# A fixed order on PE for output projection and routing, and the first context pair's product on POOL

## The chip, the cores and the metric

One core of a Trainium2 chip. The engines are PE (matrix products and transposes, into PSUM), DVE and ACT (element by element, both reach PSUM), POOL (element by element in SBUF, and indirect transfers) and SP (issues most transfers). Each engine runs its own list of instructions in order and waits at semaphores for the others. The metric is the device time of one execution in microseconds; lower is better.

## What is computed

One step of a two-layer backbone for two sets of tokens, 512 latent tokens and 128 context tokens, of width 1024. A layer is

```
x <- LN(ALPHA * x + gate1 * (mixers(modulate(x)) @ w_out))
x <- LN(ALPHA * x + gate2 * experts(modulate(x)))
```

The mixers are latent attention, a pooling mixer and a short convolution; their concatenated output (1024 wide) goes through one output projection `w_out`. The experts are 16 SwiGLU units of inner width 512: `(silu(u @ w_gate) * (u @ w_up)) @ w_down`. Routing is by choice of the experts: the router gives each token softmax weights over 16 experts, and each expert takes the tokens with the largest weights, 64 of the latent set and 16 of the context set, each set routed alone. What an expert gives for a token is scaled with that weight and added to the token's row.

## The kernel before

All numbers of lines are those of the kernel before. The 640 tokens are five tiles of 128: the context tile (CTX) and latent tiles 0 to 3. Everything below happens in each of the two layers; the places named are layer 0's.

**Output projection** (`out_proj`, from L776). `project(t, half)` (L844) makes 512 of the 1024 output columns of a tile: eight steps k, each of three products 128x512 (`mm3`, L229: inputs and weights are split in a high and a low part, `mh`/`ml` and `wo..h`/`wo..l`). The weights come as four quarters, `wo00`, `wo01` (for half 0), `wo10`, `wo11` (half 1); each is split on the way (L226 on ACT makes the high part, L227 the low part, on DVE or POOL). The sum stands in a PSUM tile `ps_o` (three buffers). DVE multiplies it with the gate (L859), adds it to the row tile `xa` (L861, in layer 1 L864) and takes statistics (L867); after half 1 it makes the mean and variance, POOL the power -0.5 (`bsd`, L285), DVE the product of mean and `bsd` (`bnb`, L322).

**Routing of a tile.** `turn(t, g)` transposes half g of `xa` on PE (L881), ACT copies it to `u2` (L883), PE multiplies it with the router's weights (L887, bank `ps_rt`). `route(t)`: ACT copies the partial sums (L896), PE folds them (L898), DVE and ACT make the softmax `rex` (L900 to L906), PE transposes it (L907), DVE copies it to `affl` (L909). ACT then normalises `xa` (L323) and stores it in DRAM as `zrow` (L911). `residual(t)` multiplies and adds on POOL (L337, L338) in place and starts the accumulator's row (L842); it has to wait for the store of `zrow`.

**Context tokens.** After the context tile's routing, `route_ctx` picks each expert's 16 tokens, two gathers (`xsc`) bring their rows, eight transposes each (`transpose8`) and a modulation on ACT (L261) give `xc`.

**End of the stage.** `route_late` (L946 on) does the last half of tile 3 with `fill(n)` between: n steps of the first pair of experts' product for context tokens (`context`, four products a step into `ps_gc`, eight steps in all). Then the top-k of the latent set on DVE (`topk`, L976 to L980, eight rounds), `route_lat` (DVE, then PE transposes the list `ldup` at L989, DVE writes the indices `lgi`, L1041) and the gather of the first pair's rows `xsl` on POOL's queue (L961).

**First pair of experts** (`experts`, j = 0): `ctx_hidden` (ACT makes `sc`, the SiLU of the gate half of `ps_gc`, L1164, for which it loads a table; DVE multiplies it with the up half, `hc`, L1166, held behind `lgi`), `ctx_turn` (PE `ps_hcT`, ACT `hcT`, L1175), `ctx_rows` (16 products into `ps_dc`, and DVE's scaling `yc`, L1187), a scatter, then `turn_x` (transposes of `xsl`) and the latent products `ps_g`, `ps_u`. The other seven pairs follow; the last context and latent results join, and the layer ends with a layer norm.

**What sets the order.** A scheduler places the instructions of each engine by its own estimate and by dependencies. In the expert stage the order on PE is fixed by hand: `inline` (L236) ties each PE instruction behind the one before (`line["pe"]`), and `line.clear()` at the start of `experts` begins this chain. In `out_proj` there is no chain, but for a few `issue_after` in `route_late`; PE's order there is the scheduler's, and it mixes `project` of neighbouring halves.

## Time and profile before

| | us |
|---|---|
| median of three runs (1268.24 to 1269.1) | 1268.43 |
| the profiled execution | 1264.65 |
| its span in the trace | 1262.9 |
| PE busy, of the span | 1180.2 (93%) |
| DVE, ACT, POOL busy | 542.2, 367.9, 252.6 |
| output projection and routing, layer 0 | 273.1 to 348.7 |
| the same, layer 1 | 870.9 to 946.5 |
| from the last routing transpose to the transposes of `xsl`, layer 0 | 348.7 to 370.2 |
| the same, layer 1 | 946.5 to 967.8 |

The times of the trace count from the start of the span. In a timeline row the first number is the start and the second the time from the first operation's start to the last one's end (an "x4" joins four operations); what stands in square brackets is how long the engine was idle ahead of it and whose work ended that. Matmul records overlap: 0.39 us is the record of one product, the next starts 0.23 us later.

### The profile page before, as it was taken

To read this page: it belongs to the slowest core of one execution; us is meant where nothing else is said; L and a number is where in the kernel's file an instruction comes from. 1 tells how busy PE (TensorE), PEld (TensorE's weight loads), DVE (VectorE), ACT (ScalarE), POOL (GpSimd) and SP (SyncE) were. 2 spreads that over 40 slices of the span, in tenths; PEclk is the share of its full clock that TensorE was granted. 3 is DMA by queue.
4 is the path that set the end of the run, shared out by engine and by line. 5 is a ranking of instruction groups with operands and counts; after the bars stand their busy time and mean duration, and the time that the engine had idled before them with its cause. 6 is when DMAs were issued, how large, how long until landed. Compare 5 with 4: busy or idle time off the path is not lost.

```text
span 1262.9 us, 18196 instructions
## 1 busy us (share of the span) xinstructions
PE 1180.2 (93%) x7244; PEld 707.2 (56%) x7244; DVE 542.2 (43%) x1266; ACT 367.9 (29%) x800; POOL 252.6 (20%) x234
## 2 busy tenths in 40 slices
...
GB/s 365 309 205 315 220 268 175 127 175 135 328 235 404 402 397 409 408 407 362 327 142 96 78 60 201 168 100 194 132 341 236 402 399 402 410 408 406 358 252 84
DMA packets 85078, 342.34 MB, mean 271 GB/s; under 512 B 18713, under 2 KB 32089, under 8 KB 54401
## 3 DMA queue, kind: packets, MB, share of 16 engines
...
q14 instruction: 29, 0.23, 0.1%
...
## 4 chain that ended last, share of the span: by engine, by line
PE 83%; DVE 7%; DMA 4%; ACT 3%; issue 1%; SPq 0%; POOL 0%; POOLq 0%; ACTq 0%; DVEq 0%
PE ps_d L239 9%; PE ps_g L239 8%; PE ps_u L239 8%; PE ps_gc L239 8%; PE ps_dc L239 4%; PE ps_ada L185 4%; PE ps_c L230 3%; PE ps_c L232 3%; PE ps_c L231 3%; PE ps_o L231 3%; PE ps_o L230 3%; PE ps_o L232 3%; DMA r_wA<-in_w_in_dram 1%; PE tr L239 1%; PE ps_p L733 1%
## 5 line engine op out<-in xcount | busy, mean ns | idle before, releaser
L239 PE MATMUL ps_d<-wd,hT 128*64 128x512 f32 x512 | 114.9, 596 | 5.0 <-DVE yc L1187 3.2
L239 PE MATMUL ps_g<-wg,xT 128*64 128x512 f32 x512 | 116.1, 595 | 0.1
L239 PE MATMUL ps_u<-wu,xT 128*64 128x512 f32 x512 | 115.3, 592 | 0.0
L239 PE MATMUL ps_gc<-wu,xc 128*32 128x512 f32 x512 | 115.0, 594 | 0.0
L239 PE MATMUL ps_gc<-wg,xc 128*32 128x512 f32 x512 | 115.0, 594 | 0.0
L1164 ACT ACTIVATE sc<-ps_gc 32x512 f32<-32x512 f32 x32 | 18.8, 588 | 304.7 <-PE ps_gc L239 276.3
L1166 DVE TENSOR_TENSOR hc<-ps_gc,sc 32x512 f32<-32x512 f32 x32 | 22.0, 688 | 175.0 <-ACT sc L1164 174.9
L239 PEld LDWEIGHTS ps_d<-wd,hT 128*64 128x64 f32 x512 | 35.9, 137 | 82.1 <-issue 77.2
L239 PEld LDWEIGHTS ps_g<-wg,xT 128*64 128x64 f32 x512 | 36.0, 137 | 75.2 <-issue 70.1
L239 PEld LDWEIGHTS ps_u<-wu,xT 128*64 128x64 f32 x512 | 37.2, 137 | 72.6 <-issue 72.6
L239 PEld LDWEIGHTS ps_gc<-wg,xc 128*32 128x32 f32 x512 | 29.2, 110 | 75.0 <-issue 74.0
L1215 DVE SCALAR_TENSOR_TENSOR ye<-ps_d,lg,gl 128x512 f32<-128x512 f32 x32 | 24.0, 751 | 99.7 <-PE ps_d L239 99.7
L185 PE MATMUL ps_ada<-wada,cs 128*32 128x512 f32 x368 | 60.2, 631 | 4.9 <-DMA wada<-in_w_ada_dram 4.8
L239 PE MATMUL ps_dc<-wd,hcT 128*32 128x512 f32 x512 | 61.0, 618 | 0.9 <-ACT hcT L1175 0.9
L1113 POOL DMA_INDIRECT yaccc<-yc,csi x28 | 39.7, 1418 | 104.1 <-DVE yc L1187 75.5
L1194 DVE TENSOR_TENSOR h<-ps_u,sg 128x512 f32<-128x512 f32 x16 | 11.1, 692 | 104.0 <-PE ps_u L239 104.0
L961 POOL DMA_INDIRECT xsl<-zrow,lgi x16 | 15.9, 994 | 167.5 <-PE tr L239 152.9
L261 ACT ACTIVATE xT<-tr,modB,modA 128x128 f32<-128x128 f32 x64 | 27.8, 457 | 27.1 <-DVE xT L264 26.6
L1113 POOL DMA_INDIRECT yacc<-ye,lgi x14 | 19.9, 1418 | 76.9 <-DVE ye L1215 44.4
L285 POOL TENSOR_TENSOR bsd<-bsd,neg_half 128x1 f32<-128x1 f32 x15 | 9.5, 636 | 127.8 <-DVE bsd L284 127.8
L239 PEld LDWEIGHTS ps_dc<-wd,hcT 128*32 128x32 f32 x512 | 15.4, 113 | 34.6 <-issue 31.8
L227 POOL TENSOR_TENSOR wo00l<-r_wo,wo00h 128x1024 fp32r<-128x1024 f32 x4 | 10.4, 2614 | 119.4 <-ACT wo00h L226 119.4
...
## 6 DMA issues: line engine op xcount, KB each, us to landing
...
```

Of the source, the lines that this page charges most:

```text
L185: nc.tensor.matmul(ps[32 * j:32 * j + 32, :], lhsT=cs[:, k, :], rhs=w[:, j * 512:(j + 1) * 512], start=(k == 0), stop=(k == KD - 1))
L230: nc.tensor.matmul(out, lhsT=lh, rhs=rh, start=first, stop=False)
L231: nc.tensor.matmul(out, lhsT=lh, rhs=rl, start=False, stop=False)
L232: nc.tensor.matmul(out, lhsT=ll, rhs=rh, start=False, stop=last)
L239: line["pe"] = op(*args, **kw)
L261: nc.scalar.activation(out=out[:, kk, :], in_=ps[:, kk, :], func=AF.Identity, scale=A[:, r, k:k + 1], bias=B[:, r, k:k + 1])
L733: nc.tensor.transpose(pt[:, kk, i * P:(i + 1) * P], prs[i][:, (k0 + kk) * P:(k0 + kk + 1) * P], ident)
L961: ins = nc.gpsimd.indirect_dma_start(out=x, out_offset=None, in_=src, in_offset=bass.IndirectOffsetOnAxis(ap=idx, axis=0))
L1113: nc.gpsimd.indirect_dma_start(out=acc[:, :], out_offset=bass.IndirectOffsetOnAxis(ap=idx[h][0:64, j:j + 1], axis=0), in_=y[hs], in_offset ...
L1164: nc.scalar.activation(out=sc[64 * i + 32:64 * i + 64], in_=pc[64 * i:64 * i + 32], func=AF.Silu)
L1166: nc.vector.tensor_tensor(out=hc[32 * i:32 * i + 32], in0=pc[64 * i + 32:64 * i + 64], in1=sc[64 * i + 32:64 * i + 64], op=ALU.mult)
L1215: order["ye"] = nc.vector.scalar_tensor_tensor(out=ye[:, hs], in0=pd, scalar=lg[:, j:j + 1], in1=gl2[:, hs], op0=ALU.mult, op1=ALU.mult)
```

## The change

The helpers of `out_proj` go through the chain of PE: `line.clear()` moves to the start of `out_proj`, `mm3` takes the function that issues, and `project` takes steps to be put between its eight k steps. The routing of a tile is cut in three places, each inside a later `project`: `match(p, 0)`, the list of the tile before and `turn(p, 1)` at k4 and `match(p, 1)` at k7 of the next tile's half 0; `weigh(p)` and `turn(t, 0)` at k4 of its half 1. The transposes of the context rows (`ctx_row`) stand at k4 of project(2, 1), k1 and k7 of project(3, 1) and in `route_late`; their modulation is now shared by DVE and ACT. In `route_late` one fill stands between the steps of tile 3, four behind the last. Then `down` issues the context pair's second product (`ctx_hidden`, `ctx_turn`, `ctx_sums`) ahead of `route_lat`'s transposes on PE. In this first pair ACT copies the up half of `ps_gc` to SBUF (`uc`), and POOL does the product `hc`. The scaling `yc` comes behind `lgi`.

```diff
 def out_proj(l, mixA, mixC, w2, ms, mixed):
+    line.clear()
...
-        def project(t, half):
+        def project(t, half, **between):
             for k in range(KD):
+                for step in between.get(f"k{k}", ()):
+                    step()
                 wh, wl = w2[2 * half + k // 4]
-                mm3(ps, mh[:, k], ml[:, k], wh[:, k % 4], wl[:, k % 4], k == 0, k == KD - 1)
+                mm3(ps, mh[:, k], ml[:, k], wh[:, k % 4], wl[:, k % 4], k == 0, k == KD - 1, mm)
...
+        def ctx_row(hf, g):
+            def step():
+                ps = ptr("tr8").rearrange("p (k n) -> p k n", k=4)
+                for kk in range(4):
+                    turn1(ps[:, kk, :], xsc[hf][:, 512 * g + kk:512 * g + 512:4], ident)
+                modulate(xc[:, 4 * g:4 * g + 4, hf * P:(hf + 1) * P], ps, A, B, 1, g)
+            return step
...
         project(CTX, 0)
-        project(CTX, 1)
-        turn(CTX, 0)
-        project(0, 0)
-        router(CTX)
...
+        project(CTX, 1, k4=[turn(CTX, 0)])
+        for t in range(4):
+            p, q = t - 1 if t else CTX, t - 2 if t > 1 else CTX
+            project(t, 0, k4=[match(p, 0)] + ([listed(q)] if t else []) + ([choose] if t == 1 else []) + [turn(p, 1)], k7=[match(p, 1)])
+            project(t, 1, k1=[ctx_row(0, 1)] if t == 3 else [], k4=[weigh(p), turn(t, 0)] + ([ctx_row(0, 0)] if t == 2 else []), k7=[ctx_row(1, 0)] if t == 3 else [])
+            if t in (1, 2):
+                residual(CTX if t == 1 else 0)
...
-        def route_late(fill):
-            ins = turn(3, 1, fill(2), lambda ins: fill(1, ins))
-            route(3, fill(1, ins))
-            fill(9, order["weighed"])
-            latr = route_lat(rt, rx, topk(rx, afl, CAPL, "ta"))
+        def route_late(fill, down):
+            match(3, 0)()
+            ctx_row(1, 1)()
+            listed(2)()
+            fill(1)
+            turn(3, 1)()
+            fill(1)
+            match(3, 1)()
+            fill(1)
+            weigh(3)()
+            fill(1)
+            listed(3)()
+            fill(4)
+            best = topk(rx, afl, CAPL, "ta")
+            pd = down()
+            with tc.issue_after(line["pe"].ins):
+                latr = route_lat(rt, rx, best)
...
-            def ctx_hidden(after=None):
+            def ctx_hidden(pool=False):
...
+                uc = newhalf("uc") if pool else None
+                for i in range(2):
+                    u = pc[64 * i + 32:64 * i + 64]
+                    if pool:
+                        u = uc[64 * i + 32:64 * i + 64]
+                        nc.scalar.copy(out=u, in_=pc[64 * i + 32:64 * i + 64])
                 for i in range(2):
+                    u = (uc if pool else pc)[64 * i + 32:64 * i + 64]
                     nc.scalar.activation(out=sc[64 * i + 32:64 * i + 64], in_=pc[64 * i:64 * i + 32], func=AF.Silu)
-                    with tc.issue_after(after.ins) if after else ExitStack():
-                        nc.vector.tensor_tensor(out=hc[32 * i:32 * i + 32], in0=pc[64 * i + 32:64 * i + 64],
-                                                in1=sc[64 * i + 32:64 * i + 64], op=ALU.mult)
+                    (nc.gpsimd if pool else nc.vector).tensor_tensor(out=hc[32 * i:32 * i + 32], in0=u,
+                                                                     in1=sc[64 * i + 32:64 * i + 64], op=ALU.mult)
...
+                def down():
+                    return ctx_sums(ctx_turn(ctx_hidden(True)), ps_dn.tile("ps_dc"))
-                (lgi, lso, lg, llast), x_first = route_late(fill)
+                (lgi, lso, lg, llast), x_first, pd = route_late(fill, down)
                 xp = opool(f"xT{l}", "left")
-                scatter(yaccc, ctx_rows(ctx_turn(ctx_hidden(order["lgi"]))), csi, j)
+                with tc.issue_after(order["lgi"].ins):
+                    yc = ctx_scaled(pd)
+                scatter(yaccc, yc, csi, j)
```

`turn`, `match`, `weigh` and `listed` hold the instructions of the old `turn` and `route`, and `choose` those of `route_ctx` and its two gathers. `ctx_sums` and `ctx_scaled` are the two parts of the old `ctx_rows`.

Three places show what this does to the engines' orders.

PE at the head of the output projection, before: `ps_o_2966` is the sum of project(CTX, 1), `ps_o_3015` that of project(0, 0).

```order
L232 MATMUL ps_o_2937<-wo01h0_2817,ml_2494 128x512
L230 MATMUL ps_o_2966<-wo10h0_2835,mh_2493 128x512
L230 MATMUL ps_o_3015<-wo00h0_2050,mh_2826 128x512
L231 MATMUL ps_o_3015<-wo00l0_2051,mh_2826 128x512
L232 MATMUL ps_o_3015<-wo00h0_2050,ml_2827 128x512
```
After the first product of project(CTX, 1) PE goes over to the next tile. After the change, at the middle of project(CTX, 1) (`xa_2935` is the context tile):

```order
L239 MATMUL ps_o_2966<-wo10h0_2835,mh_2493 128x512
L239 MATMUL ps_o_2966<-wo10l0_2836,mh_2493 128x512
L239 MATMUL ps_o_2966<-wo10h0_2835,ml_2494 128x512
L239 MATMUL tr8_2979<-ident_72,xa_2935 128x128 x4
L239 MATMUL ps_o_2966<-wo11h0_2844,mh_2493 128x512
L239 MATMUL ps_o_2966<-wo11l0_2845,mh_2493 128x512
L239 MATMUL ps_o_2966<-wo11h0_2844,ml_2494 128x512
```
All twelve products with `wo10` stand ahead of the transposes of the context tile's first half, and these stand ahead of the products with `wo11` and of the next tile.

PE at the end of the routing, before: the last filling products, the list (`ps_tc`), then the context pair's transposes and second product.

```order
L239 MATMUL ps_gc_3619<-wg0_1_1_3603,xc0_2880 32x512
L239 MATMUL ps_gc_3619<-wu0_1_1_3607,xc0_2880 32x512
L989 MATMUL ps_tc_3719<-ident_72,ldup_3717 128x16
L989 MATMUL ps_tc_3732<-ident_72,lvd_3730 128x16
L239 MATMUL ps_hcT_3750<-ident_72,hc_3744 128x64 x4
L239 MATMUL ps_dc_3756<-wd0_0_0_3609,hcT_3749 32x512 x2
L239 MATMUL ps_dc_3756<-wd0_1_0_3611,hcT_3749 32x512 x2
```
After the change, first behind the last filling products and then at the list:

```order
L239 MATMUL ps_gc_3599<-wg0_1_1_3583,xc0_2880 32x512
L239 MATMUL ps_gc_3599<-wu0_1_1_3587,xc0_2880 32x512
L239 MATMUL ps_hcT_3720<-ident_72,hc_3711 128x64 x4
L239 MATMUL ps_dc_3726<-wd0_0_0_3589,hcT_3719 32x512 x2
L239 MATMUL ps_dc_3726<-wd0_1_0_3591,hcT_3719 32x512 x2
```
And where `ps_dc` ends:

```order
L239 MATMUL ps_dc_3726<-wd0_0_1_3593,hcT_3719 32x512 x2
L239 MATMUL ps_dc_3726<-wd0_1_1_3595,hcT_3719 32x512 x2
L1006 MATMUL ps_tc_3752<-ident_72,ldup_3750 128x16
L1006 MATMUL ps_tc_3765<-ident_72,lvd_3763 128x16
L239 MATMUL tr8_3781<-ident_72,xsl_3770 128x128 x4
L239 MATMUL tr8_3790<-ident_72,xsl_3770 128x128 x4
L239 MATMUL ps_g_3600<-wg0_0_0_3573,xT_3780 64x512
```
The list's transposes have moved from ahead of `ps_hcT` to behind the last product into `ps_dc`.

POOL at the end of the routing, before: `bsd_3519` belongs to tile 3, `xa_3275` to tile 2, `xa_3424` to tile 3, `xsl_3737` is the first pair's gather.

```order
L285 TENSOR_TENSOR bsd_3519<-bsd_3519,neg_half_77 128x1
L337 TENSOR_TENSOR xa_3275<-xa_3275,ln1_g_0_2885 128x1024
L338 TENSOR_TENSOR xa_3275<-xa_3275,ln1_b_0_2888 128x1024
L961 DMA xsl_3737<-zrow_95,lgi_3721 128x1024
L337 TENSOR_TENSOR xa_3424<-xa_3424,ln1_g_0_2885 128x1024
```
After the change (`bsd_3511` tile 3, `xa_3264` tile 2, `xa_3386` tile 3):

```order
L337 TENSOR_TENSOR xa_3264<-xa_3264,ln1_g_0_2885 128x1024
L338 TENSOR_TENSOR xa_3264<-xa_3264,ln1_b_0_2888 128x1024
L285 TENSOR_TENSOR bsd_3511<-bsd_3511,neg_half_77 128x1
L843 DMA yacc_98<-xa_3264 128x1024
L1188 TENSOR_TENSOR hc_3711<-uc_3712,sc_3710 32x512 x2
L978 DMA xsl_3770<-zrow_95,lgi_3754 128x1024
L337 TENSOR_TENSOR xa_3386<-xa_3386,ln1_g_0_2885 128x1024
```
The residual of tile 2 has moved ahead of `bsd` of tile 3, and the two products `hc` stand ahead of the gather.

## Rows read from the trace of the kernel before

**Rows 1.** Windows from start to end of the stage, layers 0 and 1: busy us by engine

```profile
273.10:348.70 75.60, 73.82 (x429) 56.16 (x427) 47.19 (x114) 32.80 (x64) 21.00 (x16) 1.00 0.66 243
870.90:946.50 75.60, 73.84 (x429) 56.14 (x427) 46.91 (x114) 32.77 (x64) 20.98 (x16) 1.00 0.66 243
```

**Rows 2.** Timeline of PE, layer 0's tail: start us, us, operation, [idle before <-releaser]

```profile
338.32 0.39 PE L232 MATMUL ps_o<-wo11h,ml 128*128 128x512 f32 x1
...
346.60 0.40 PE L898 MATMUL ps_rt<-fold,parts 128*128 128x16 f32 x2
...
348.74 0.28 PE L907 MATMUL ps_rt<-ident,rex 128*16 128x128 f32 x1 [1.62 <-DVE rex L906]
...
360.46 0.28 PE L989 MATMUL ps_tc<-ident,ldup 16*128 16x16 f32 x1 [7.88 <-DVE ldup L1036]
...
364.01 0.71 PE L239 MATMUL ps_hcT<-ident,hc 64*128 64x64 f32 x4 [1.81 <-DVE hc L1166]
365.18 5.12 PE L239 MATMUL ps_dc<-wd,hcT 128*32 128x512 f32 x32 [0.46 <-ACT hcT L1175]
370.23 1.24 PE L239 MATMUL tr<-ident,xsl 128*128 128x128 f32 x8
```

**Rows 3.** Timeline of POOL, layer 0's tail

```profile
341.42 0.55 POOL L285 TENSOR_TENSOR bsd<-bsd,neg_half 128x1 f32<-128x1 f32 x1 [11.35 <-DVE bsd L284]
349.84 2.40 POOL L337 TENSOR_TENSOR xa<-xa,ln_g 128x1024 f32<-128x1024 f32 x1 [7.87 <-DMA zrow<-xa]
...
361.41 1.05 POOL L961 DMA_INDIRECT xsl<-zrow,lgi  x1 [6.76 <-DVE lgi L1041]
```

**Rows 4.** Landing of layer 1's first two gathers of `xsl`

```profile
DMA to landing us min/median/max: 4.5/6.8/9.1
```

**Rows 5.** Timeline of PE, head of layer 0's output projection

```profile
278.83 0.39 PE L230 MATMUL ps_o<-wo10h,mh 128*128 128x512 f32 x1
279.06 0.39 PE L230 MATMUL ps_o<-wo00h,mh 128*128 128x512 f32 x1
```

**Rows 6.** Timeline of DVE, head of layer 0's output projection

```profile
278.37 1.21 DVE L227 TENSOR_TENSOR wo10l<-r_wo,wo10h 128x1024 fp32r<-128x1024 f32 x1
...
279.71 1.22 DVE L227 TENSOR_TENSOR wo10l<-r_wo,wo10h 128x1024 fp32r<-128x1024 f32 x1
...
281.65 2.35 DVE L227 TENSOR_TENSOR wo11l<-r_wo,wo11h 128x1024 fp32r<-128x1024 f32 x2
283.91 0.68 DVE L861 SCALAR_TENSOR_TENSOR xa<-xa,ps_o 128x512 f32<-128x512 f32 x1
```

**Rows 7.** Timeline of all engines, middle of layer 0's stage

```profile
311.36 2.38 POOL L338 TENSOR_TENSOR xa<-xa,ln_b 128x1024 f32<-128x1024 f32 x1
311.44 2.85 DVE L227 TENSOR_TENSOR ml<-mixA,mh 128x512 fp32r<-128x512 f32 x1
```

**Rows 8.** Timeline of DVE, layer 0's tail

```profile
338.00 0.48 DVE L1276 TENSOR_SCALAR hot<-hot,clast 128x128 f32<-128x128 f32 x2 [2.94 <-DMA hot<-in_k_iota_dram]
...
371.05 1.81 DVE L264 TENSOR_SCALAR xT<-tr,modA,modB 128x128 f32<-128x128 f32 x4
```

**Rows 9.** Timeline of ACT: layer 0's attention, and its routing's end

```profile
218.90 1.28 ACT L679 ACT_TABLE_LOAD   x1 [3.32 <-DVE mx L677]
220.20 0.79 ACT L679 ACTIVATE pr<-sc,mx 128x640 f32<-128x640 f32 x1
...
348.23 1.28 ACT L1164 ACT_TABLE_LOAD   x1
352.65 0.59 ACT L1164 ACTIVATE sc<-ps_gc 32x512 f32<-32x512 f32 x1 [3.13 <-PE ps_gc L239]
```

**Rows 10.** The page's groups: `ps_dc`, mean over all

```profile
L239 PE MATMUL ps_dc<-wd,hcT 128*32 128x512 f32 x512 | 61.0, 618 | 0.9 <-ACT hcT L1175 0.9
```

**Rows 11.** Windows of 2 us at layer 0's hole; the eighth column is PEclk

```profile
358.00:360.00 2.00, 0.00 (x0) 0.00 (x0) 1.84 (x10) 0.00 (x0) 0.00 (x0) 0.50 0.02 4
...
368.00:370.00 2.00, 2.00 (x20) 0.36 (x12) 0.00 (x0) 0.00 (x0) 1.61 (x2) 0.95 0.62 131
```

131 lines of the change are left out of this document (58 added, 73 removed).

## The prediction

> **What bounds the kernel now.** I read the page's busy times and the windows by stage first. PE is at work for 73.8 of the 75.6 us of layer 0's output projection and routing, and the same in layer 1 [rows 1]: only 1.8 us of PE idling are there to be won in that stage. The hole lies behind it, between the last routing transpose (348.74) and the first expert pair's transposes (370.23), in both layers. Its largest piece is the wait of the list transpose for `ldup`, the end of DVE's top-k chain: 7.88 us [rows 2]. Then PE stands at the context pair's product (`ps_hcT`, `ps_dc`, 364.01 to 370.23), and only at its end come the transposes of the gathered rows `xsl` [rows 2]. That gather was issued at 361.41 and its like lands in 4.5 us [rows 3, 4], so at 365.9 the rows were there and PE took them 4.3 us late. The change goes at this: the pair's product is to move into the wait for the list. In the expert stage behind, I take PE as the bound, so what the two stages lose or win reaches the end one to one, twice.
>
> **The change, part by part, per layer (times on layer 0's axis).**
>
> *Head.* Before, PE started one product with `wo10h` at 278.83 and then went on with the next tile (`wo00h`, 279.06), since `wo10l` was not there [rows 5]. DVE makes `wo10l` in two parts that end at 278.37 + 1.21 = 279.58 and 279.71 + 1.22 = 280.93 [rows 6]. Now PE's order holds all of project(CTX, 1) first. Its second product waits from 279.06 to 279.58: 0.5 us. Eleven more at 0.227 us (two neighbours are 0.23 apart [rows 5]) bring PE to 282.1, where `turn(CTX, 0)` stands. That needs the context tile's first half of `xa`, which DVE ends at 283.91 + 0.68 = 284.59, because both parts of `wo11l` (281.65, 2.35 us) stand ahead of it on DVE [rows 6], and DVE's order there is unchanged. 284.6 - 282.1 = 2.5 us. Head: **+3.0**, between 2.5 and 3.1; nothing else is in PE's order that could fill it.
>
> *Middle.* A `turn(t, 1)` now stands 12 products (2.7 us) behind the end of its half, and DVE's multiply and add need 1.4 us (0.7 each [rows 6])), which leaves 1.3. DVE's split `ml` reads two operands in SBUF; it took 2.85 us where POOL's residual product ran beside it (311.36, 2.38 us) [rows 7], 2.2 more than the 0.68 of an operation of that size [rows 6]. POOL's residuals now stand earlier. One split caught costs 2.2 - 1.3 = 0.9, two 1.8, none 0: I take **+0.5**. Splitting the modulation of `xc` between DVE and ACT and cutting the routing in three places moves short work beside long products; I put nothing for it.
>
> *Tail.* Let E be the end of the last projection (338.32 + 0.23 before [rows 2])). The first filling products need the PSUM bank that DVE frees: multiply 0.7, two modulations of 0.45 each (1.81 for four [rows 8])) that now stand between, add 0.7, in all E + 2.4. PE has about 1.0 us of short work till then (two groups of four like the 0.71 of `ps_hcT`, overlapped, and one transpose): 1.4 idle. Then turn(3,1), match(3,1), weigh(3) and four fills alternate to E + 6.9, weigh(3) at E + 5.9. From weigh to listed it was 348.74 - 346.60 = 2.14 us [rows 2], and two operations on `hot` (0.48 together [rows 8])) now stand in that chain on DVE: listed(3) at E + 8.5, idle 1.6. Tail idle 3.0, less the 1.8 that the stage had: **+1.2**; between -0.6 (only 1.2 of the chain uncovered) and +1.5.
>
> *From listed(3), called L, to `xsl`.* Filling ends as before, when ACT may read the sums, at 352.65 - 348.74 = L + 3.9 [rows 9]. Then in a row: two copies of the u half (0.59 each by the size of `sc`) to 5.1; the table load (1.28) which was hidden under the filling and now stands behind the copies, to 6.4; `sc` twice, to 7.0 and 7.5; POOL's two products on 32x512. POOL shows no such operation: 0.55 us on 128x1 and 2.40 on 128x1024 [rows 3] bound it, and halfway, 1.4 each, is my value: 9.8. Transposes, copy and start of `ps_dc` took 365.18 - 364.01 = 1.2, so `ps_dc` starts at L + 11.1 and by its 5.05 us [rows 2] ends at L + 16.1. DVE's list is ready at L + 11.7 as before (360.46 - 348.74), but its transpose stands behind `ps_dc` on PE: 4.4 us late. From it to the gather's issue 0.95 [rows 2, 3], landing 4.5 [rows 4], hence `xsl` transposes at L + 21.7. Before: 370.23 - 348.74 = 21.5. So the 4.3 us by which PE took the rows late are not won; they are moved ahead of the gather: **+0.2**. Bounds: POOL at 0.55 each and `ps_dc` at its mean of 61.0/16 = 3.8 us [rows 10] give -2.7; POOL at 2.40 gives +2.2.
>
> Behind the table load ACT starts at once: load at 218.90 + 1.28, next operation at 220.20 [rows 9]. The Trainium skill (ScalarE: Activation LUTs, What ACT_TABLE_LOAD costs) puts a drain of 1.38 us on top, 2.66 in all. Here the measurement decides, and it shows no drain behind the load; by the page the sum below would be 2 x 1.38 = 2.8 us more, 1281.0.
>
> *Sum.* 3.0 + 0.5 + 1.2 + 0.2 = 4.9 us per layer, 9.8 for two. The profiled execution took 1264.65 us, which gives 1274.45; it lies 3.8 us under the median of the runs, 1268.43, and on that scale the forecast is **1278.2 us**. All terms at their ends give -0.8 and +8.6 per layer: 1266.8 and 1285.6.
>
> **The rivals.**
>
> 1. *The pair's product is over early, and the tail does not wait* (faster). If POOL needs 0.55 each and `ps_dc` runs in 3.8 us, the last part is -2.7; if in the tail PE finds each short step ready (DVE's bank free at E + 1.0, the chain covered by the fills), the 1.8 us of before are gone too. 3.0 - 1.8 - 2.7 = -1.5 per layer: 1265.4. It decides where POOL's product falls under about 0.8 us. For it: 32 partitions and half the row are little work. Against: the clock at the place, 0.50 from 358 until PE has worked for some us [rows 11], which makes `ps_dc` long, and the chain of weigh, which is in no way shorter. Chance 0.12.
>
> 2. *Gain and loss cancel* (no change). The last part at -2.7, the tail at 0, middle at 0: +0.3 per layer, 1269.0. For it speaks only that the two ends with the least evidence both fall well. 0.13.
>
> 3. *POOL's queue and the clock* (slower still). POOL's residual of tile 2 now stands ahead of `bsd` of tile 3, and it waits for tile 2's store of `zrow`: 7.87 us of waiting before [rows 3], when nothing hung on it. By my walk the store is issued at about 335.8, lands about 344, the two products of 2.4 us end at 349, and `bsd` is wanted at 350.7. If the store lands 3.5 us later, listed(3) is 2 us later. Also PE now idles twice for some 5.5 us instead of once for 7.9, with `ps_dc` between. The granted clock was at 0.50, the level of 1.2 GHz, when PE had stood idle, and `ps_dc` took 5.05 instead of 3.8 us for it [rows 2, 10, 11]; if the first pair's products start at that level again, another 1.3 us. Together +3.3 per layer on the forecast's 4.9: 1284.8. Chance 0.13. The Trainium skill (TensorE: Matmul & The Clock Gate, HAM oscillation) describes this repeated cost, bursts between waits that each begin slow; no row of before shows two such holes in a row.
>
> **How the numbers follow.** The forecast, slower by 5 to 14 us, has 0.62, since the head's waits rest on rows of DVE whose order is not changed. About 0.2% (2.5 us) is what a measurement of this kernel can tell from no change. Faster by more 0.12 (rival 1), within 0.13 (rival 2), slower 0.62 + 0.13 = 0.75. The range of 8 in 10 runs from 1266 to 1285: it takes in the ends of the sum but for rival 1's better half, and rival 3.
>
> **What would show it.** Head: in the changed trace a PE wait of about 2.5 us for DVE's add to `xa` and one of 0.5 for `wo10l`, in both layers. Tail: a PE wait of about 1.4 for the same kind of add, one of about 1.6 for `rex`. End: PE's first `ps_tc` transpose directly behind `ps_dc`, with `ldup` some 4 us older, and 21 to 22 us between listed(3) and the `xsl` transposes. If POOL's products are shorter than 0.8 us, or the head's wait is missing because DVE's add comes ahead of `wo11l`, I am wrong towards rivals 1 and 2; if `bsd` of tile 3 waits on POOL behind a store, towards rival 3. It is also wrong if the expert stage, here taken as bound by PE, gives time back.

## The result, and the profile after

The changed kernel takes 1300.5 us (median; 1297.5 to 1304.7) against 1268.8 for the kernel before on the same chip: a ratio of **1.0249, 95% interval 1.0212 to 1.0285**, 31.8 us slower. The forecast was 1278.2, with a range of 1266 to 1285. The sign was right; the loss is three times the one forecast and lies outside the range. The profiled execution took 1302.84 us, its span is 1301.1; the spans of the two profiles are 38.2 us apart, more than the medians, since the profile of before is one of its shorter executions and that of after one of its longer ones.

Three stretches of each layer tell where it went: the stage of the output projection and routing (to L, the last routing transpose, as in the prediction), from L to the first `xsl` transposes, and from there to the join, PE's first `ps_z` product.

| us, layer 0 / layer 1 | before | after |
|---|---|---|
| stage, to L | 75.6 / 75.6 | 84.2 / 81.5 |
| L to `xsl` transposes | 21.5 / 21.3 | 24.2 / 24.3 |
| `xsl` transposes to join | 259.0 / 257.7 | 262.2 / (join moved) |
| `xsl` transposes to PE's last four products | - / 275.7 | - / 290.4 |

Layer 0 loses 8.6 + 2.7 + 3.2 = 14.5 us and layer 1 5.9 + 3.0 + 14.7 = 23.6. Before the first stage the profile of after is 2.4 us late, and between the layers it gains 2.3: together the 38.2 us by which the spans differ. The 2.4 are not of the change: over all the kernels below, which are the same up to there, the profiles begin that stage between 273.1 and 276.9.

The stage, answering [rows 1] (busy us of PE, PEld, DVE, ACT, POOL, then PEclk, DMA share, GB/s):

```profile
275.60:359.80 84.20, 76.14 (x429) 56.16 (x428) 51.79 (x122) 30.97 (x55) 26.24 (x19) 0.98 0.62 224
885.50:966.90 81.40, 74.62 (x429) 54.98 (x427) 51.22 (x122) 31.05 (x55) 26.18 (x19) 1.00 0.61 225
```

In layer 0 PE's work grew from 73.8 to 76.1 us, though it does the same products, and it idles 8.1 us instead of 1.8; in layer 1 it is 74.6 of work and 6.8 idle. The head, answering [rows 5, 6], on PE and then on DVE:

```profile
282.06 0.50 PE L239 MATMUL ps_o<-wo10l,mh 128*128 128x512 f32 x1 [0.42 <-DVE wo10l L227]
...
287.11 0.72 PE L239 MATMUL tr<-ident,xa 128*128 128x128 f32 x4 [2.27 <-issue]
```

```profile
282.13 1.22 DVE L227 TENSOR_TENSOR wo10l<-r_wo,wo10h 128x1024 fp32r<-128x1024 f32 x1
...
284.06 2.35 DVE L227 TENSOR_TENSOR wo11l<-r_wo,wo11h 128x1024 fp32r<-128x1024 f32 x2
286.33 0.68 DVE L865 SCALAR_TENSOR_TENSOR xa<-xa,ps_o 128x512 f32<-128x512 f32 x1
```

Both waits of the prediction stand there, 0.42 for `wo10l` (forecast 0.5) and 2.27 until DVE's add to `xa` is done at 287.01 (forecast 2.5; the profile writes "issue" for it). What was not in the sum is what comes behind, in the windows that answer [rows 11]:

```profile
285.00:287.00 2.00, 0.00 (x0) 0.00 (x0) 2.00 (x3) 0.00 (x0) 0.00 (x0) 1.00 0.86 360
287.00:289.00 2.00, 1.89 (x8) 1.64 (x9) 0.71 (x2) 0.59 (x1) 0.00 (x0) 0.78 0.97 299
289.00:291.00 2.00, 2.00 (x6) 1.63 (x5) 0.00 (x0) 0.00 (x0) 0.00 (x0) 0.50 0.75 315
291.00:293.00 2.00, 2.00 (x9) 1.58 (x9) 0.79 (x2) 1.01 (x2) 0.00 (x0) 0.86 0.00 0
```

The granted clock falls to 0.50, the level of 1.2 GHz, after the wait, and the twelve products with `wo11`, from 287.58 to 292.01, take 4.4 us where twelve at 0.227 take 2.7: 1.7 us more. It does not always do so. In layer 1 of the same profile PE waits as long, and the clock stays at 1.00:

```profile
897.04 0.72 PE L239 MATMUL tr<-ident,xa 128*128 128x128 f32 x4 [2.24 <-issue]
```

```profile
897.00:899.00 2.00, 1.96 (x11) 1.73 (x12) 0.67 (x1) 0.59 (x1) 0.00 (x0) 1.00 0.92 258
899.00:901.00 2.00, 2.00 (x10) 1.68 (x9) 0.44 (x1) 0.67 (x2) 0.00 (x0) 1.00 0.80 332
```

Most of the 2.8 us by which layer 1's stage is shorter than layer 0's is this. The middle, answering [rows 7], has one wait per layer that is worth naming, of 1.08 and 1.03 us, ahead of a `turn`:

```profile
319.71 3.42 DVE L227 TENSOR_TENSOR ml<-mixA,mh 128x512 fp32r<-128x512 f32 x1
323.05 0.67 DVE L865 SCALAR_TENSOR_TENSOR xa<-xa,ps_o 128x512 f32<-128x512 f32 x1
```

```profile
323.78 0.75 PE L239 MATMUL tr<-ident,xa 128*128 128x128 f32 x4 [1.08 <-DVE xa L865]
```

It is the one the prediction described: POOL's residual product (L338) runs from 320.17 to 322.57, beside the split `ml`, which takes 3.42 us and holds up the add to `xa`. The tail and the hole, answering [rows 2], PE and then POOL [rows 3]:

```profile
351.33 0.62 PE L239 MATMUL ps_gc<-wg,xc 128*32 128x512 f32 x1 [0.99 <-DVE xa L865]
...
359.78 0.38 PE L239 MATMUL ps_rt<-ident,rex 128*16 128x128 f32 x1 [3.30 <-DVE rex L912]
...
371.18 0.74 PE L239 MATMUL ps_hcT<-ident,hc 64*128 64x64 f32 x4 [5.92 <-POOL hc L1188]
372.38 5.84 PE L239 MATMUL ps_dc<-wd,hcT 128*32 128x512 f32 x32 [0.46 <-ACT hcT L1197]
378.16 0.23 PE L1006 MATMUL ps_tc<-ident,ldup 16*128 16x16 f32 x1
...
383.93 1.98 PE L239 MATMUL tr<-ident,xsl 128*128 128x128 f32 x8 [4.13 <-DMA xsl<-zrow,lgi]
```

```profile
351.66 2.37 POOL L337 TENSOR_TENSOR xa<-xa,ln_g 128x1024 f32<-128x1024 f32 x1 [11.56 <-DMA zrow<-xa]
354.11 2.37 POOL L338 TENSOR_TENSOR xa<-xa,ln_b 128x1024 f32<-128x1024 f32 x1
356.43 0.55 POOL L285 TENSOR_TENSOR bsd<-bsd,neg_half 128x1 f32<-128x1 f32 x1
...
368.54 2.58 POOL L1188 TENSOR_TENSOR hc<-uc,sc 32x512 f32<-32x512 f32 x2 [10.98 <-issue]
379.53 1.04 POOL L978 DMA_INDIRECT xsl<-zrow,lgi  x1 [8.41 <-issue]
...
384.11 0.09 POOL L1090 MEMSET wg<- 1x1 f32 x1
```

PE stands 0.99 us for `xa` (forecast 1.4), 3.30 for `rex` (forecast 1.6; 2.15 in layer 1), 5.92 for POOL's `hc`, and 4.13 for the gathered rows. That `rex` is late comes from POOL: DVE waits for `bsd` of tile 3, which stands on POOL behind the two residual products.

```profile
357.02 0.16 DVE L322 SCALAR_TENSOR_TENSOR bnb<-bmv,bsd 128x1 f32<-128x1 f32 x1 [3.95 <-POOL bsd L285]
```

PE's part of the routing of tile 3 (`ps_rt<-fold,parts`) was done at 355.48, `bsd` at 356.98, 1.5 us behind it; in layer 1 it was 0.4 behind. `ps_dc` runs 5.84 us, and the list's transpose stands directly behind it, as forecast. In the last layer the join has moved:

```profile
1250.52 3.75 PE L1329 MATMUL ps_z<-z,ident 128*128 128x512 f32 x4 [11.52 <-DMA z<-yacc]
```

PE waits here 11.52 us for `z`, ahead of the last pair's `ps_hT`, which in the kernel before stood at 1214.10, 11.4 us before its join.

### The profile page after: what moved, and what is told of

Same layout as the page of the kernel before. It is cut to its first block, busy times and chain, and to the rows that moved or that the text cites. A ratio compares the mean times of both kernels' runs of the same rounds, so it can differ in the third digit from the quotient of the medians.

```text
span 1301.1 us, 18201 instructions
## 1 busy us (share of the span) xinstructions
PE 1194.8 (92%) x7244; PEld 710.2 (55%) x7244; DVE 547.0 (42%) x1278; ACT 366.8 (28%) x788; POOL 257.4 (20%) x238
## 5 line engine op out<-in xcount | busy, mean ns | idle before, releaser
L239 PE MATMUL ps_gc<-wg,xc 128*32 128x512 f32 x512 | 118.7, 609 | 2.0 <-DVE xa L868 1.0
L239 PE MATMUL ps_gc<-wu,xc 128*32 128x512 f32 x512 | 118.7, 609 | 0.0
L1188 DVE TENSOR_TENSOR hc<-ps_gc,sc 32x512 f32<-32x512 f32 x28 | 19.2, 687 | 173.8 <-ACT sc L1187 173.7
L239 PEld LDWEIGHTS ps_d<-wd,hT 128*64 128x64 f32 x512 | 35.7, 137 | 84.2 <-issue 77.4
L264 DVE TENSOR_SCALAR xT<-tr,modA,modB 128x128 f32<-128x128 f32 x64 | 25.1, 408 | 26.4 <-PE tr L239 16.3
L337 POOL TENSOR_TENSOR xa<-xa,ln_g 128x1024 f32<-128x1024 f32 x10 | 23.7, 2374 | 55.8 <-DMA zrow<-xa 28.4
## 6 DMA issues: line engine op xcount, KB each, us to landing
wu<-in_w_up_dram SPq DMA_DIRECT2D x64, 1024.0 KB, 21.7
```

What stands on the lines that cost most here:

```text
L239: line["pe"] = op(*args, **kw)
L264: nc.vector.tensor_scalar(out=out[:, kk, :], in0=ps[:, kk, :], scalar1=A[:, r, k:k + 1], scalar2=B[:, r, k:k + 1], op0=ALU.mult, op1=ALU.add)
L337: nc.gpsimd.tensor_tensor(out=out, in0=zh, in1=L["g"], op=ALU.mult)
L1188: (nc.gpsimd if pool else nc.vector).tensor_tensor(out=hc[32 * i:32 * i + 32], in0=u, in1=sc[64 * i + 32:64 * i + 64], op=ALU.mult)
```

## Taking the change back piece by piece

Each of these starts from the kernel named. Most change one thing more; where one changes several (e10, e13, e15, e17, e18), they are named. The table gives all the runs; each was timed beside the kernel before on its chip.

| run | median us | ratio to before, 95% interval |
|---|---|---|
| e1_join | 1295.0 | 1.0228 (1.0204 to 1.0253) |
| e2_join_head | 1286.1 | 1.0151 (1.0108 to 1.0194) |
| e3_join_oldend | 1281.9 | 1.0127 (1.0104 to 1.0151) |
| e4_down_alone | 1276.9 | 1.0094 (1.0069 to 1.0119) |
| e5_down_warm | 1309.1 | 1.0323 (1.0303 to 1.0343) |
| e6_list_inside | 1307.4 | 1.0315 (1.0294 to 1.0336) |
| e7_tail | 1276.2 | 1.0075 (1.0053 to 1.0097) |
| e8_hoist | 1276.4 | 1.0066 (1.0045 to 1.0088) |
| e9_down_warm2 | 1281.0 | 1.0109 (1.0086 to 1.0132) |
| e10_best | 1280.1 | 1.0098 (1.0074 to 1.0121) |
| e11_before_warm | 1276.1 | 1.0070 (1.0049 to 1.0091) |
| e12_down_warm3 | 1272.8 | 1.0050 (1.0033 to 1.0067) |
| e13_best3 | 1273.8 | 1.0064 (1.0042 to 1.0086) |
| e14_best3_bare | 1274.1 | 1.0060 (1.0038 to 1.0082) |
| e15_best4 | 1272.2 | 1.0040 (1.0023 to 1.0056) |
| e16_best4_bare | 1276.7 | 1.0073 (1.0056 to 1.0091) |
| e17_late_gate | 1267.1 | 1.0003 (0.9988 to 1.0018) |
| e18_best5 | 1262.5 | 0.9968 (0.9955 to 0.9982) |

**e1_join**, after with the join's products tied behind the chain of PE:

```diff
-            put = mm if t < 2 else nc.tensor.matmul
+            def late(*args, **kw):
+                with tc.issue_after(tail.ins):
+                    return nc.tensor.matmul(*args, **kw)
+            put = mm if t < 2 else late
+        tail = line["pe"]
```

> The changed kernel, but the joins' first products of tile 2 in the last layer (ps_z<-z, which the scheduler put ahead of ps_hT and ps_d of the last pair) are tied behind the last context product, as in the kernel before. Theory 'PE's order at the end': the 11.5 us of waiting for z go, and about 1.5 us of slow clock behind it, because z lands while PE works on ps_d: 1300.5 - 13 = 1287.5 (1285 to 1290). Rival 'scatters': the wait is POOL's late last scatter, whose landing z's load waits for; then PE only waits a few products later, and the time stays over 1297.

The stretch from the `xsl` transposes to PE's last four products falls from 290.4 to 281.4 us in the profiles, but the ratio only by 0.0021, some 2.7 us, and the intervals overlap. **e8_hoist** puts the same early join, with the loads of `z` that it needs, into the kernel before:

```diff
+                if l + 1 == a["depth"]:
+                    z2, zs = [], []
+                    zs += [load_z(t) for t in range(2)]
...
+                    early = [ptr("ps_z") for n in range(2)]
+                    for n in range(2):
+                        mm(early[n], lhsT=ident, rhs=zs[2][:, n * 512:n * 512 + 512], start=True, stop=False)
```

> The kernel before with one thing of the changed one: in the last layer the two products ps_z<-z of tile 2 stand ahead of the last pair's ps_hT and ps_d. Theory 'PE's order at the end': z lands at about 1221, PE is there at 1214; 7 us of waiting and 2 of slow clock, 7 to 11 us more than before. Rival: z comes in time on an undelayed kernel, under 3 us more.

It costs 9.3 us there. So the join is a real part of the loss, of 3 to 9 us. In the profiles, e1 wins 9.0 us in this stretch and gives back 3.2 ahead of it: 1.0 in layer 0's stretch to the join, and 1.6 and 0.6 in layer 1's stage and hole. The 1.6 are the half clock at the head, which e1 pays in both layers and after, in the profiled execution, in one. How much of the rest is chance from one execution to the next stays open.

**e2_join_head**, e1 with the head's order of before:

```diff
-        project(CTX, 1, k4=[turn(CTX, 0)])
+        project(CTX, 1)
-            project(t, 0, k4=[...], k7=[match(p, 1)])
+            project(t, 0, k1=[turn(CTX, 0)] if t == 0 else [], k4=[...], k7=[match(p, 1)])
```

> As e1_join, and turn(CTX, 0) moves from k4 of project(CTX, 1) to k1 of project(0, 0). Theory 'head': the wait of 2.3 us for xa goes, and the 3 to 4 us at half clock behind it, about 1.7 us: 4.0 per layer, 8 us less than e1_join (6 to 9). Rival 'moved': what the head saves is waited for later, in the routing's chain at the end of the stage; then within 3 us of e1_join.

The ratio falls by 0.0077, 9.8 us, 4.9 per layer. In the profiles the stage is 3.9 and 4.0 us shorter than e1's: the wait for `xa` is gone, waits of 0.6 us for `wo10l` and `wo11l` stay, so 2.0 us less waiting, and the half clock of 1.7 us is gone. What the ratio gives over that is less than the intervals can tell.

**e7_tail**, e2 with the four last fills ahead of `listed(3)`:

```diff
             weigh(3)()
-            fill(1)
-            listed(3)()
             fill(4)
+            listed(3)()
+            fill(1)
```

> As e2_join_head, but four of the five last filling steps stand ahead of listed(3) and one behind it. Theory 'tail wait': PE's wait of 2.2 to 3.3 us for rex is covered, the filling runs at full clock, and ps_hcT comes some 3 us earlier after listed(3): 3 to 4 us per layer, 6 to 8 us less than e2. Rival 'chain': the last fills only put listed(3) and the top-k later; then within 2 us of e2.

In layer 0 PE's wait for `rex` falls from 3.55 to 0.67 us, the stage is 0.2 and 0.5 us longer with three more fills done, the `xsl` transposes stand at L + 19.1 and 19.8 instead of 24.5 and 22.9, and the ratio falls by 0.0076, 9.6 us. What is left, 9.5 us, is of the size of the new end alone (e4 below), but is not shown to be that alone: stage and hole together are still 2.8 and 2.5 us longer than before, and the stretch to the join 2.7 and 4.3.

**e3_join_oldend**, e1 with the end of before (DVE's `hc`, the list ahead of the pair):

```diff
-            pd = down()
-            with tc.issue_after(line["pe"].ins):
-                latr = route_lat(rt, rx, best)
+            latr = route_lat(rt, rx, best)
+            pd = None
```

> As e1_join, but the end of the stage as in the kernel before: the list's transposes first, then hc on DVE behind lgi, ps_hcT, ps_dc. Theory 'list behind ps_dc': from the last routing transpose to the transposes of xsl it is 21.5 again instead of 24.2, 2.8 per layer, 5.5 us less than e1_join (4 to 7). Rival 'clock': the end is as long whatever its order, since PE idles as long in all; within 1.5 us of e1_join.

The old end wins 0.0101, 12.8 us, where the prediction put 0.4 on the end; the stretch from `xsl` to join is back at 257.7 in both layers. **e4_down_alone** asks the other way round, the new end alone on the stage of before (as in after: `ctx_hidden(True)`, `ctx_turn`, `ctx_sums` ahead of `route_lat`; the join in its old place):

```diff
-            latr = route_lat(rt, rx, topk(rx, afl, CAPL, "ta"))
+            best = topk(rx, afl, CAPL, "ta")
+            pd = down()
+            with tc.issue_after(line["pe"].ins):
+                latr = route_lat(rt, rx, best)
```

> The kernel before with only the new end: copies of the u half, product on POOL, ps_dc ahead of the list. Output projection as before. Theory 'list behind ps_dc': +2.7 per layer, 1268.8 + 5.4 = 1274.2 (1272 to 1277). Rival 'late routing': the new end was late only because the stage before it ended late and cold; then 1266 to 1270.

10.8 us slower. The stages are 75.6 us as before, the `xsl` transposes come at L + 22.3 and 22.0, but the join 262.5 and 262.2 us behind them. So the expert stage, which I took as rigid, gives away 4 us per layer (3.5 and 4.5).

## Is it the clock? Products without use in PE's waits

Here PE does products whose results nobody reads, in its waits (nothing that is computed changes). First the stretch in question, in windows of its first 15 us, its middle and its last 40, for before (first and last), e4 and after (layers 1, 1 and 0):

```profile
967.82:982.82 15.00, 14.97 (x76) 5.55 (x72) 2.30 (x5) 2.43 (x5) 3.21 (x3) 1.00 1.02 407
1185.50:1225.50 40.00, 40.00 (x235) 12.99 (x233) 8.15 (x15) 4.09 (x9) 7.02 (x5) 1.00 0.92 318
```

```profile
972.41:987.41 15.00, 15.00 (x66) 5.92 (x68) 1.55 (x4) 2.32 (x5) 7.23 (x7) 0.88 0.97 352
987.41:1194.61 207.20, 204.82 (x1258) 72.49 (x1258) 38.77 (x71) 26.40 (x59) 34.59 (x27) 1.00 1.02 401
1194.61:1234.61 40.00, 38.33 (x212) 11.79 (x205) 6.43 (x10) 2.35 (x5) 6.95 (x5) 1.00 0.89 306
```

```profile
383.93:398.93 15.00, 15.00 (x66) 5.90 (x68) 1.55 (x4) 3.38 (x6) 7.30 (x7) 0.89 0.98 348
398.93:606.13 207.20, 204.10 (x1256) 72.42 (x1256) 39.73 (x78) 27.16 (x60) 34.53 (x26) 1.00 1.02 401
606.13:646.13 40.00, 38.49 (x216) 11.83 (x208) 6.38 (x10) 2.55 (x5) 6.99 (x5) 1.00 0.93 311
```

In e4 and after the first pair runs at a clock of 0.88 and 0.89, 1.7 us lost of 15; in the last 40 us PE idles 1.67 and 1.51 us, which is a wait for weights (`ps_d <- DMA wd`). Before has neither in layer 1; in layer 0 it waits 0.26 us for weights.

**e5_down_warm**, e4 and these products (24 in the wait for `hc`, 17 in that for `xsl`):

```diff
+                def warm(n):
+                    for _ in range(n):
+                        mm(pg[0:64, :], lhsT=xc[:, 0, 0:64], rhs=w["g", 0, 0][:, 0, :], start=True, stop=True)
...
+                    warm(24)
...
+                warm(17)
```

> As e4_down_alone, with products without use on PE (into ps_g, which the next real product starts anew): 24 between the filling and ps_hcT, 17 between the list and the transposes of xsl, so that PE does not idle there. They add nothing to what is computed. Theory 'clock': what e4 loses behind the transposes of xsl (4.6 us per layer) and in ps_dc is mostly PE at half clock after its two idle stretches; ps_dc takes 3.8 instead of 5 us, the first pair 2 us less: 7 us less than e4, 2 to 5 us over the kernel before. Rival 'transfers': the loss is late weights and late copies of hT; then within 2 us of e4, 9 to 12 over the kernel before.

**e6_list_inside** puts the list's transposes between `ps_dc`'s products besides:

```diff
+                    warm(20)
+                    hcT = ctx_turn(hc)
+                    pd = ctx_sums(hcT, ps_dn.tile("ps_dc"), range(2))
+                    listed(lambda: (ctx_sums(hcT, pd, range(2, 4)), warm(3)))
+                    warm(15)
```

> Output projection as before; the new end changed at three points: ACT makes sc of a half first and copies its u behind it, so that the table load stays under the filling; the list's transpose stands in the middle of ps_dc (behind 8 of 16 products), and products without use fill PE's waits (20 and 15). Theory 'the order of the end': list at L + 11.7 as before, gather at once, xsl transposed at L + 17.5 instead of 21.5 at full clock: 4 us per layer, 8 us less than the kernel before (5 to 9). Rival 'not the first pair': the expert stage starts when the weights behind the gather come; then within 2 us of the kernel before.

Both are some 40 us slower and decide little of the total: a product took 0.87 us, twice what was meant, and outlasted the waits. Within e5 `ps_dc` took 3.64 us and the stretch to the join 255.8. The next three were sized by 0.43 us again, which is one record, where a product is two. **e9_down_warm2** is e5 with `warm(12)` and `warm(8)`:

> e4_down_alone (the new end alone, on the order of before) with products added whose results nobody reads: 12 of them on PE in the wait for POOL's hc, 8 in the wait for the xsl rows. One took 0.43 us in e5_down_warm, so 12 are 5.2 us against a wait of 5.9, and 8 are 3.4 us against a wait of 3.5: this time they should not outlast the waits. Theory, half clock behind waits: ps_dc falls from 5.84 to about 3.65, the list's transpose comes at L + 15 instead of L + 17.1, the xsl transposes at L + 20, and the expert stage from there to the join takes 256 to 258 us instead of 262.5. Per layer 276 to 278 against before's 280: 4 to 8 us faster than before in all, where e4 was 10.75 slower. Rival, the gather's and the weights' transfers are late or DVE and ACT are: the expert stage stays at 262 and the sum is 9 to 12 us slower than before.

**e10_best** has an end of its own (ACT's `sc` and `uc` half by half, residuals behind the gather):

```diff
+                    hc = ctx_hidden(True)
+                    warm(9)
+                    hcT = ctx_turn(hc)
+                    pd = ctx_sums(hcT, ps_dn.tile("ps_dc"), range(3))
+                    listed(lambda: (ctx_sums(hcT, pd, range(3, 4)), warm(1)))
+                    warm(8)
...
-                    residual(t, order["last"].ins if t == 3 else None)
+                    residual(t, order["last"].ins if t > 1 else None)
```

> Before's order of the output projection, the join where it was, and the new end put together in another way: ACT makes sc and then uc half by half, so that the table load lies under the filling; 9 products without use cover the wait for POOL's hc; 12 of ps_dc's 16 products run, then the list's transpose, then the last 4, then the lvd transpose, then 8 products without use until the xsl rows land; POOL's residuals of tiles 2 and 3 start behind the gather's issue. Theory (the list behind ps_dc, the table load in the open and the half clock were what the new end lost): list's transpose at L + 12, as DVE's top-k chain allows, xsl transposes at L + 17.4 instead of 21.5, expert stage at 257 to 258: 4 to 5 us per layer, 8 to 10 us faster than before. Rival, what the end gains the expert stage gives back because something else than PE sets its pace (weights, DVE's split of the rows): stage at 262, within 2 us of before.

**e11_before_warm** has `warm(17)` in the kernel before, ahead of `route_lat`:

> The kernel before with nothing but 17 products without use on PE in its wait of 7.88 us for the list (17 times 0.43 = 7.3 us). It prices the half clock behind a wait by itself. Theory: ps_dc behind the wait takes 3.65 us instead of 5.05, and nothing else moves: 1.4 us per layer, 2.8 us in all (1.5 to 4) faster than before. Rival, the half clock of that place is hidden by something else that is late: within 1 us of before. If the products outlast the wait, the list's transpose is late by what they are over.

All three lose 9 to 14 us and their totals decide nothing; the products are still too long (e9, timeline of PE):

```profile
353.19 10.51 PE L239 MATMUL ps_g<-wg,xc 128*64 128x512 f32 x24
...
364.79 3.64 PE L239 MATMUL ps_dc<-wd,hcT 128*32 128x512 f32 x32 [0.46 <-ACT hcT L1185]
```

12 of them, 24 records, take 10.51 us. But e9's stretch to the join is clean:

```profile
376.93:391.93 15.00, 14.98 (x73) 5.55 (x72) 1.64 (x4) 2.58 (x6) 4.19 (x4) 1.00 1.02 380
391.93:595.49 203.56, 200.55 (x1226) 70.91 (x1224) 37.91 (x74) 25.86 (x56) 34.53 (x26) 1.00 1.02 402
595.49:635.49 40.00, 40.00 (x236) 12.86 (x234) 8.14 (x15) 4.09 (x9) 6.99 (x5) 1.00 0.99 341
```

No half clock, no idling in the last 40 us, 258.6 us. That could be the clock, or that the `xsl` transposes came so late here (L + 27.5) that all weights were there. **e12_down_warm3** has 6 and 4, which fit the waits:

```diff
-                    warm(12)
+                    warm(6)
-                warm(8)
+                warm(4)
```

> e9_down_warm2 with half the products whose results nobody reads: 6 in the wait for POOL's hc and 4 in the wait for the xsl rows. In e9 12 of them took 10.51 us and 8 took 7.08, 0.88 us each (each stands as two records of 0.44 us in the trace, which I had counted as one product), so 6 are 5.3 us against a wait of 5.9 and 4 are 3.5 against one of 3.5. Theory, half clock behind waits: ps_dc 3.65 us instead of 5.84 and the expert stage 258 us as in e9 (258.6 and 257.9) instead of 262.5 in e4, with the xsl transposes at L + 21 instead of L + 22.2: 5 to 6 us per layer less than e4, so about the time of before (-3 to +2 us). Rival, e9's stage was short because its gather came so late that weights and rows were all there, not for the clock: the stage is back at 262 and the sum stays 9 to 12 us above before.

It wins 0.0044 on e4, 5.6 us, half of what the clock theory gave. `ps_dc` takes 3.64 us, the `xsl` transposes come 1.3 and 0.6 us sooner and layer 1's stretch is 259.8; but in layer 0 it is 264.2, for a wait on PE that ACT's row explains:

```profile
392.71 7.50 PE L239 MATMUL ps_d<-wd,hT 128*64 128x512 f32 x26 [3.73 <-ACT hT L1216]
```

```profile
390.65 1.06 ACT L333 ACTIVATE ln_b<-ln_b 128x1024 f32<-128x1024 f32 x1 [6.04 <-DMA ln_b<-in_ln_b_dram]
...
392.29 0.37 ACT L1216 COPY hT<-ps_hT 128x256 f32<-128x256 f32 x1
```

ACT's operation on the next layer norm's rows, whose load waits for POOL's late residual of tile 3, stands ahead of `hT`. Behind this wait the granted clock falls too (0.74 from 392 to 396), and all 32 records of this `ps_d` take 8.78 us where the kernel before needs 7.09. In the kernel before the same row ended its wait at 383.63, before `hT` was wanted.

## The end mended, and the weight stream

**e13_best3** is e10 with fewer products without use and POOL's residual of tile 2 ahead of `hc`; **e14_best3_bare** is e13 without the two lines `warm(4)`:

```diff
-                    hc = ctx_hidden(True)
-                    warm(9)
+                    hc = ctx_hidden(residual(2))
+                    warm(4)
...
-                    warm(8)
+                    warm(4)
```

> e10_best with the products without use cut from 9 to 4 (wait for hc) and from 8 to 4 (wait for xsl), the one between the list's two transposes left out, and POOL's residual of tile 2 put ahead of hc, that of tile 3 behind the gather as in the kernel before (in e10 both stood behind the gather, and the loads of the next layer norm's rows, which wait for them, held ACT's operations up by 2.26 us at the first pair's hidden rows). Theory: list's transpose at L + 12, xsl transposes at L + 17.5 instead of before's 21.5, expert stage 258: 4 us per layer, 6 to 10 us faster than before. Rival, the expert stage is paced by something that does not move with the gather: it takes 261 to 262 and the time is within 2 us of before.

> e13_best3 without the products whose results nobody reads, and nothing else changed: what the order by itself brings. Theory, half clock behind waits: PE waits some 4 us for hc, ps_dc runs at half clock, the list's transpose comes at L + 13 to 14, PE waits some 3.5 us for xsl, and the expert stage takes 262: 4 to 6 us per layer more than e13, so about the time of before (-2 to +4 us). Rival, the products change nothing: the same time as e13 within 2 us.

They take the same time: in e13 the `xsl` transposes come 2.6 and 1.4 us sooner, and layer 0's stretch behind them is 1.9 us longer, 1.6 of it a second wait for `yc`. The four products do not fill e13's wait for `hc` either (2.55 and 2.41 us stay). **e15_best4** (against e10) clears POOL's and ACT's queues as well, with `warm(4)` twice; **e16_best4_bare** is e15 without these:

```diff
-                for t in (1, 2, 3):
-                    residual(t, order["last"].ins if t > 1 else None)
+                for t in (1, 2):
...
+                residual(3, order["last"].ins)
...
-                nc.scalar.activation(out=res[n], in_=res[n], func=AF.Copy, scale=ALPHA)
+                with tc.issue_after(order["hT"].ins) if "hT" in order else ExitStack():
+                    nc.scalar.activation(out=res[n], in_=res[n], func=AF.Copy, scale=ALPHA)
```

> e13_best3 with POOL and ACT re-ordered: both residuals (tiles 2 and 3) behind the gather on POOL, so that hc is not late and no POOL product runs beside DVE's last list operations (in e12 two of these took 1.89 and 2.39 us instead of 0.18 and 0.21), the second residual behind the second gather, and ACT's two operations on the next layer norm's rows behind the second pair's hT, so that hT of the first pair no longer stands behind their load (in e12 PE waited 3.73 us there, 0.78 in the kernel before). The 4 and 4 products without use stay. Theory, clock plus these two queues: list's transpose at L + 12, xsl transposes at L + 17.5, expert stage 257 to 258 in both layers: 4 us per layer, 6 to 9 us faster than before. Rival, something else sets the expert stage's end: 260 to 262, and within 2 us of before.

> e15_best4 without the products whose results nobody reads. Theory: PE waits about 4 us for hc and 3.5 for xsl, ps_dc runs at half clock, the list's transpose comes at L + 13.5 and the xsl transposes at L + 18.5, the expert stage begins at half clock and takes 260: 3 us per layer more than e15, so 0 to 4 us faster than before. Rival, the products change nothing (as between e13 and e14): the same time as e15 within 2 us.

The front is now won as computed, the list at L + 11.8, the `xsl` transposes at L + 17.5, 4 us before those of before. And the whole gain is given back in the stretch behind, which takes 264.5 and 264.4 us, 5.5 and 6.7 more than before's: 1.6 of it is a second wait for `yc`, and the most is lost at its end:

```profile
609.73 3.65 PE L239 MATMUL ps_u<-wu,xT 128*64 128x512 f32 x14 [1.16 <-DMA wu<-in_w_up_dram]
...
623.02 5.36 PE L239 MATMUL ps_d<-wd,hT 128*64 128x512 f32 x22 [1.48 <-DMA wd<-in_w_down_dram]
```

PE waits for weights, 2.65 us in the last 40 of layer 0 and 2.74 in layer 1. e16 is 4.2 us slower than e15, which prices what the products without use save in this order: 2 us per layer. In all the runs so far the weight loads stand still in the hole, until a MEMSET of one element on POOL, behind the gathers of the first two pairs and whatever else POOL has there, lets SP issue the next (in before SP issues it at 366.11):

```profile
365.99 0.09 POOL L1074 MEMSET wg<- 1x1 f32 x1
```

**e17_late_gate** moves this MEMSET in the kernel before. It also moves ACT's two operations on the next layer norm's rows out of the way, as e15 does:

```diff
-                with tc.issue_after(order["gather"].ins):
+                with tc.issue_after(order["kept"].ins):
                     nc.gpsimd.memset(t[0:1, 0, 0:1], 0.0)
```

> The kernel before with one POOL instruction moved: the MEMSET of one element (L1074) behind which SP may issue the first weight load after the hole stands behind POOL's residual of tile 3 and its store, not behind the second gather; by the rows of before that is 369.9 instead of 365.99, L + 21.2 instead of L + 17.2. PE's and DVE's orders are those of before, row for row (ACT's two operations on the next layer norm's rows come two pairs later, so that they are in nobody's way). Theory, the weight stream: in all kernels so far ps_z stands 262 us behind this MEMSET (259 to 264.6 in 16 of 18), whatever PE did, so the list's and the xsl transposes stay at L + 11.7 and L + 21.4, PE then waits for weights late in the stage, and ps_z comes at L + 283 instead of 280.5 and 279.0: 3 to 4 us per layer, 5 to 8 us slower than before. Rivals, PE with its clock, or the list, set the stage's end: nothing that these wait for has moved, so within 1 us of before.

```profile
366.95 2.37 POOL L339 TENSOR_TENSOR xa<-xa,ln_b 128x1024 f32<-128x1024 f32 x1
...
370.18 0.09 POOL L1075 MEMSET wg<- 1x1 f32 x1
```

The MEMSET stands at 370.18 instead of 365.99, and the time is the same: my theory in the form "join = MEMSET + 262" falls. The weights have some slack in the kernel before. Over the runs it fits that where the MEMSET comes 3 us or more ahead of the `xsl` transposes (before, e3, e5, e6, e8, e9, e11) PE waits 0 to 0.3 us for weights in the last 40 us, but for 1.06 in one layer of e8, and where it comes between 1.1 ahead and 2.7 behind, PE waits 0 to 3.1 us; in both layers over 2.6 only in e15 and e16, the latest two. The limit isn't sharp: e17, at 0.6 and 1.8 ahead, has no such wait, e12 and e13, at 0.2 behind to 0.3 ahead, have 0 to 0.3, and e10 at 1.1 ahead has 2.88 in one layer. **e18_best5** is e15 with the MEMSET directly behind the first gather:

```diff
+                w_next = pair_weights(1)
+                for t in (2, 3):
+                    residual(t, order["gate"].ins)
-                residual(3, order["last"].ins)
```

> e15_best4 with the same MEMSET directly behind the first gather on POOL, ahead of both residuals and of the second gather: L + 13.8 instead of L + 20.1. Theory, the weight stream: ps_z 262 us behind it is L + 276 if the weights do not hold up the gather, 277 to 278 if the gather's rows, now beside the weights, land 1 to 2 us later; e15 had L + 282.0 in both layers and before 280.5 and 279.0. So 8 to 12 us faster than e15 and 4 to 8 us faster than before. Rival, the stage's end was set by PE and its order in e15, not by the weights: the same time as e15 within 2 us, 4 to 5 us slower than before.

```profile
362.41 1.03 POOL L965 DMA_INDIRECT xsl<-zrow,lgi  x1 [5.35 <-issue]
363.49 0.09 POOL L1079 MEMSET wg<- 1x1 f32 x1
363.67 4.66 POOL L338 TENSOR_TENSOR xa<-xa,ln_g 128x1024 f32<-128x1024 f32 x2
```

It takes 1262.5 us against 1266.0, ratio 0.9968 (0.9955 to 0.9982): **faster than both kernels**, by 0.3% than the one before, and 9.1 us faster than e15, in which PE has the same steps in the same order. Laid over each other from the `xsl` transposes on, the PE records of the two are within 0.02 us for 230 us; the 4.0 and 4.6 us by which e18, counted from there, is at its join sooner arise behind that, where e15 waits for weights. No wait for weights is left, and the stretch to the join takes 260.5 and 259.8. That is 1.5 and 2.1 us longer than before's; 1.6 of it is the second wait for `yc`, and the 0.5 more in layer 1 stays open. POOL's residuals moved with the MEMSET, so what is shown is that the place on POOL decides, not the one instruction alone. The early MEMSET in the kernel before was not run; there PE waits 0.26 us and nothing for weights, so little is to be won.

## Why the prediction was right in sign and wrong in size

The forecast was 4.9 us per layer; the profile of after shows 14.5 in layer 0 and 23.6 in layer 1. The waits of the walk were there, most of them near their size. Two steps failed: the price of a wait, taken at its length, and the sentence that PE bounds the expert stage. The join at the program's end was not in the sum at all.

*Head, forecast 3.0 per layer: 4.4 and 2.7 in the profile, 4.9 by e2.* The waits were right to 0.3 us (2.7 in both layers). The step that failed is their price: I took a wait at its length, and in layer 0 PE came out of 2.27 us of it at half clock, which cost 1.7 us. In layer 1 it did not; there the term came out nearly as forecast, and by luck, since e1 and e3 pay the half clock in both layers.

*Middle, forecast 0.5: 1.1 and 1.0.* The mechanism was right, with one split caught per layer, which the prediction had put at 0.9.

*Tail, forecast 1.2: 2.5 and 1.3 of waiting, and 1.7 of half clock behind it in both layers; e7 wins 4.8.* The waits were seen, but that for `rex` was 3.30 and 2.15 instead of 1.6. A part of rival 3 came true: POOL's residual of tile 2 waited for its store (11.56 us), and `bsd` of tile 3 stood behind it until 356.43. The walk had the residual's products end 1.7 us before `bsd` was wanted; in the trace they end at 356.48, 1.0 us after PE's part was done. The fills behind `listed(3)` then ran at half clock, and all of it lay in front of `hc`. e7 shows that this order was a choice: with the fills in the wait most of the loss is gone. The remaining 0.7 and 0.8 us of the stage's loss lie in PE's busy time, and the trace does not split them further; the prediction put nothing for the short steps that now stand between long products.

*End, forecast 0.2: 2.7 and 3.0 in the hole, and 3.2 in layer 0's expert stage* (e4, the end alone, costs 10.8 us in both layers together, 5.4 each). POOL's two products took 2.58 us (forecast 2.8), and the order on PE is the one of my walk. `xsl` came at L + 24.2 (L + 22.3 in e4) instead of 21.7 (the walk's own terms add up to 21.6), by the filling and `ps_dc` at half clock (1.7 and 0.7 us in after). The larger error is the sentence "I take PE as the bound, so what the two stages lose or win reaches the end one to one". The gather came 7.1 us later behind L (379.53 - 359.78 against 12.7), and with it the MEMSET that frees the weight loads; their slack was used up, and PE waited for weights at the end of the stretch, 1.5 us. The first pair began at half clock besides, 1.7 us. My own walk had the list's transpose, and so the gather, 4.4 us late: the wait was in the numbers, but I asked only when the rows would be there for PE, not what else hangs on POOL's place.

*The join, not forecast: 3 to 9 us in all.* The scheduler moved two products of the join, which the chain of PE doesn't hold, ahead of the last pair. I had compared the orders only where the diff is.

Of the rivals, 1 and 2 needed short steps that did not come; 3 had the mechanisms (store, half clock) and 1284.8, still 16 us short. The Trainium skill (TensorE: Matmul & The Clock Gate, HAM oscillation) describes bursts between waits that each begin slow; layer 0's trace agrees, with a clock of 0.50 behind each of the waits of 2.27, 3.30, 5.92 and 4.13 us, and in layer 1 the wait of 2.24 us is the exception. Where the Trainium skill (ScalarE: Activation LUTs, What ACT_TABLE_LOAD costs) puts a drain on top of the table load, the row of after again shows none behind it:

```profile
365.33 1.17 ACT L1184 COPY uc<-ps_gc 32x512 f32<-32x512 f32 x2 [6.08 <-PE ps_gc L239]
366.52 1.28 ACT L1187 ACT_TABLE_LOAD   x1
367.81 1.20 ACT L1187 ACTIVATE sc<-ps_gc 32x512 f32<-32x512 f32 x2
```

366.52 + 1.28 is 367.80, and `sc` starts at 367.81. So the measurement was the right choice there.
